# Attention scores of the four head pairs in two 64-row halves of the array, with one transposed copy of q and k

## The chip, the cores and the metric

One core of a Trainium2 chip runs the whole program. The metric is the device time of one execution in microseconds (us); lower is better. The engines have one queue of instructions each: TensorE (PE) multiplies, with a separate row of weight loads (PEld) in the profile; VectorE (DVE) and ScalarE (ACT) work element by element; GpSimd (POOL) does little here; SyncE (SP) issues the weight transfers. Matmul results land in PSUM, eight banks of 128 partitions by 512 fp32.

## The reference

Two transformer layers on 512 tokens of width 1024, in fp32. The first layer's attention is the one that changes: eight heads, each with two components of 64 features, whose softmaxes are subtracted.

```python
def diff_attention(h, cos, sin, w_qkv, q_norm, k_norm, lam_p, subln, w_o, layer_idx):
    q, k, v = jnp.split(h @ w_qkv, [DA_QK, 2 * DA_QK], axis=-1)
    q = apply_rope(rms_norm(q.reshape(B, S, DA_HEADS, 2, HEAD_DIM), q_norm), cos, sin)
    k = apply_rope(rms_norm(k.reshape(B, S, DA_HEADS, 2, HEAD_DIM), k_norm), cos, sin)
    ...
        s = jnp.einsum('bqhcd,bkhcd->bhcqk', qblk, k).astype(jnp.float32) * scale
        p = jax.nn.softmax(jnp.where(causal, s, NEG_INF), axis=-1)
        a = p[:, :, 0] - lam * p[:, :, 1]
        return jnp.einsum('bhqk,bkhe->bqhe', a.astype(v.dtype), v)
    ...
    o = rms_norm(o, subln) * (1.0 - lambda_init)
    return o.reshape(B, S, DA_V) @ w_o
```

Then come a SwiGLU FFN, the second layer (a window attention of 16 query heads on four shared key heads, window 128) and its FFN.

## The kernel before

Every product is made of two parts per operand, a value rounded to fp32r (hi, the suffix h) and the rest (lo, l), and of three matmuls, hi x hi, hi x lo and lo x hi. A split is a ScalarE cast to hi and a VectorE subtraction for lo; weights pass through it too (`parts`, L278 and L279).

The tokens are four blocks of 128. The first layer's heads go by pairs: `Pair` p has two heads, so four 64-feature components for q and four for k. For each pair `gemm` makes 512 columns of q and k for all blocks (L300 to L302 into four acc banks), then 256 of v. `rope` on VectorE turns a block's 512 columns into td, and multiplies the k half by its gains and norms into kd (L417), with each component of k twice, the second copy made by ScalarE (L419). The pair's steps are then:

- K (`turn_k`): four transposes of kd (L426) and their split into kT (L447 ScalarE, L448 VectorE).
- Q (`turn_q`): two transposes of td and their split into q (L436, L437, two steps each of 64 partitions), which stacks a component's hi above its lo in 128 rows; then the next block's rope.
- C (`score`): per component two matmuls, stacked q against kT hi twice (L809) and against kT lo twice (L810). One sc bank takes two components of up to 256 columns, or one of 384 or 512. Then VectorE adds the mask and takes the row maximum (L814, with a second short instruction, both named mx in the waits). The last C of a block starts `soften`: exponentials on ScalarE (L827), sums and the subtraction of the second softmax on VectorE (L835).
- U (`turn`): transposes of the weights (L851) and their split (L306, L307). W (`weigh`): the products with v. N (`norm`) and B (`spread`): the rms norm over heads and its way back.

The order of TensorE's work is written by hand: `DA_STEPS` gives each step a slot, `DA_STEPS3` for the last pair, and between two steps the loop pulls as many matmuls of the next pair's q, k and v (for the last pair, of the output projection) as the slots' distance times `DA_FILL` allows. ScalarE's and VectorE's order comes from priorities: a block under `tc.high_priority(offset=...)` is put ahead by that offset (BOOST for weight splits, EVAC for splits and reductions out of PSUM, HOT and NPRI for others). A pair's last steps run inside the next pair's.

PSUM has four acc banks, two tr banks for everything transposed (and for two of the FFN's sums), one sc and one po. Whoever takes a bank waits until its last reader is done. The second layer's attention has its own `score` (L1120, L1121), with the same stacked q and the sc bank, and its own list of slots (`SW_AT`, six for each of 16 units).

Of the kernel before, what the change touches and what calls it, by code (L numbers as in the profile page):

```python
# [9 lines left out]
F32 = mybir.dt.float32  # L10
# [7 lines left out]
P = 128  # L18
# [11 lines left out]
BOOST = 40  # L30
HOT = 610
EVAC = 20
# [6 lines left out]
NPRI = 1538  # L39
DA_FILL = 0.6361  # L40


def DA_STEPS(K, Q, C, U, W, N, B):
    return [
        (0, Q, 0),
        (0, K, 0),
        (5, C, 0, (0, 1)),
        (5.3, K, 1),
        (5.4, Q, 1),
        (6.5, C, 0, (2, 3)),  # L50
        (7.8, K, 2),
        (9.1, C, 1, (0, 1)),
        (11, C, 1, (2, 3)),
        (12.3, Q, 2),
        (13.5, U, 0, 1),
        (16.8, C, 2, (0,)),
        (17.5, U, 0, 0),
        (17.8, C, 2, (1,)),
        (18.4, K, 3),
        (19, C, 2, (2,)),  # L60
        (19, Q, 3),
        (20, C, 2, (3,)),
        (21, U, 1, 0),
        (21, C, 3, (0,)),
        (21.1, W, 0, 0),
        (23.1, U, 1, 1),
        (24.5, C, 3, (1,)),
        (28.5, W, 0, 1),
        (29, C, 3, (2,)),
        (30.5, N, 0),  # L70
        (31.9, C, 3, (3,)),
        (32.5, U, 2, 0),
        (38.3, B, 0),
        (38.8, U, 2, 1),
        (41.8, U, 3, 0),
        (42.8, U, 3, 1),
        (43, W, 1, 0),
        (43.1, W, 1, 1),
        (49, N, 1),
        (58.9, B, 1),  # L80
    ]


def DA_STEPS3(K, Q, C, U, W, N, B):
    return [
        (0, K, 0),
        (0, Q, 0),
        (3, K, 1),
        (3, C, 0, (0, 1)),
        (5, Q, 1),  # L90
        (6, C, 0, (2, 3)),
        (8, K, 2),
        (10, C, 1, (0, 1)),
        (12.5, C, 1, (2, 3)),
        (13, Q, 2),
        (13.5, U, 0, 0),
        (14.5, C, 2, (0,)),
        (15, U, 0, 1),
        (16.2, C, 2, (1,)),
        (18.5, K, 3),  # L100
        (19, C, 2, (2,)),
        (19, Q, 3),
        (20.3, C, 2, (3,)),
        (21.6, C, 3, (0,)),
        (22.4, U, 1, 1),
        (23.5, U, 1, 0),
        (25, C, 3, (1,)),
        (26.3, W, 0, 0),
        (27.3, W, 0, 1),
        (28.3, C, 3, (2,)),  # L110
        (30.9, N, 0),
        (31.4, C, 3, (3,)),
        (35.8, U, 2, 1),
        (38.2, U, 2, 0),
        (38.3, B, 0),
# [3 lines left out]
        (42.8, W, 1, 1),  # L119
        (48.5, N, 1),  # L120
        (57.5, B, 1),
# [3 lines left out]
DA_FILL3 = 0.468  # L125
# [22 lines left out]
def tile_yoco_hybrid(  # L148
# [44 lines left out]
    def att(tag="tr"):  # L193
        return ps.tile([P, 512], F32, name=nm(tag), tag=tag, bufs=2 if tag == "tr" else 1)
# [1095 lines left out]
```

## Time and profile before

| | us |
|---|---|
| median of 3 runs (lowest, highest) | 1179.5 (1178.88, 1181.27) |
| the profiled execution | 1179.42 |
| its span, first to last instruction | 1177.6 |
| PE busy | 1141.6 |
| DVE busy | 858.3 |
| ACT busy | 599.7 |

In time, the stages are: the start and the first pair's projections up to 46 us; the four pairs' attention from 46 to 258; the first FFN up to 635; the second layer's projections and attention from 635 to 822; the second FFN to the end. A matmul's row in the trace is longer than the distance to the next, since they are pipelined: 512 columns show 0.39 us and start 0.23 apart. So busy time of PE is not work at its peak, and distances between starts say more than durations. Idle time ahead of an instruction is put down to the wait that ended last.

### The profile page before, as it was taken

How to read it: one execution, taken by the hardware profiler on the slowest of the kernel's cores; microseconds unless marked ns; L12 is line 12 of the kernel's file. 1: busy time of each engine (PE TensorE's matmuls, PEld its weight loads, DVE VectorE, ACT ScalarE, POOL GpSimd, SP SyncE). 2: the span in 40 equal slices, each digit the busy share in tenths (PEclk: the TensorE clock that was granted, in tenths of full speed). 3: DMA queues.
4: the chain of work that ended last, by engine and by line, in shares of the span. 5: the costliest groups of instructions: out<-in, count | busy, mean ns of one | idle time of the engine just before them, and what ended most of it. 6: DMA issues, size and time to landing. Idle time of an engine off the chain costs nothing.

```text
span 1177.6 us, 16518 instructions
## 1 busy us (share of the span) xinstructions
PE 1141.6 (97%) x5910; PEld 963.7 (82%) x5910; DVE 858.3 (73%) x2084; ACT 599.7 (51%) x1259; POOL 16.9 (1%) x32
## 2 busy tenths in 40 slices
PE   8999999899999999999999999989999999999998
PEld 7888788678988888888888888767988888888887
DVE  5989898979776477467567697988777568468446
ACT  6676756554434343343346579788443343344333
POOL 0100000000000000000002000000000000000000
PEclk9999999999999999999999999999999999999999
DMA  6311121113524215206302211120605206305301
GB/s 189 108 54 55 54 61 62 59 54 86 183 74 144 70 57 178 89 1 216 106 1 75 90 58 51 37 72 1 222 29 193 94 1 210 94 19 179 108 1 71
DMA packets 86579, 103.14 MB, mean 88 GB/s; under 512 B 5161, under 2 KB 68034, under 8 KB 86498
## 3 DMA queue, kind: packets, MB, share of 16 engines
q1 hardware_dynamic: 86064, 100.97, 26.7%
q0 software_dynamic: 384, 1.11, 0.4%
q8 instruction: 46, 0.75, 0.3%
q14 instruction: 35, 0.29, 0.1%
q10 hardware_dynamic: 50, 0.01, 0.0%
HBM read 99.98 MB, written 2.10 MB: 87 GB/s over the span
## 4 chain that ended last, share of the span: by engine, by line
PE 75%; DVE 14%; ACT 7%; DMA 2%; issue 1%; SPq 0%; DVEq 0%; ACTq 0%
PE acc L300 17%; PE acc L302 17%; PE acc L301 17%; PE acc L597 15%; PE tr L597 3%; ACT s L1139 2%; DVE q L437 1%; ACT s L1146 1%; DVE s L814 1%; DMA raw<-in_da_w_qkv_dram 1%; DVE hss L393 1%; DVE lo L279 1%; DVE kT L448 1%; DVE td L412 1%; DVE u L409 1%
## 5 line engine op out<-in xcount | busy, mean ns | idle before, releaser
L301 PE MATMUL acc<-hTl,hi 128*128 128x512 f32 (+1 forms) x768 | 285.4, 372 | 1.2 <-DVE hTl L307 1.2
L300 PE MATMUL acc<-hTh,hi 128*128 128x512 f32 (+1 forms) x768 | 285.5, 372 | 0.0
L302 PE MATMUL acc<-hTh,lo 128*128 128x512 f32 (+1 forms) x768 | 285.2, 371 | 0.0
L278 ACT CAST hi<-raw 128x512 fp32r<-128x512 f32 x256 | 154.5, 621 | 249.8 <-PE acc L301 119.9
L279 DVE TENSOR_TENSOR lo<-raw,hi 128x512 fp32r<-128x512 f32 x256 | 172.9, 687 | 104.5 <-ACT hi L278 104.0
L578 ACT CAST hi<-g 128x512 fp32r<-128x512 f32 x154 | 95.6, 622 | 160.6 <-PE acc L301 99.2
L301 PEld LDWEIGHTS acc<-hTl,hi 128*128 128x128 f32 x768 | 144.7, 188 | 26.6 <-DVE hTl L307 1.7
L300 PEld LDWEIGHTS acc<-hTh,hi 128*128 128x128 f32 x768 | 144.7, 188 | 24.9
L302 PEld LDWEIGHTS acc<-hTh,lo 128*128 128x128 f32 x768 | 144.7, 188 | 24.9
L579 DVE TENSOR_TENSOR lo<-g,hi 128x512 fp32r<-128x512 f32 x154 | 104.6, 687 | 70.6 <-ACT hi L578 70.6
L300 PE MATMUL acc<-hi,hTh 128*128 128x256 f32 (+1 forms) x384 | 137.5, 358 | 3.6 <-ACT hTh L306 1.5
L302 PE MATMUL acc<-hi,hTl 128*128 128x256 f32 (+1 forms) x384 | 130.5, 340 | 0.3 <-DVE hTl L307 0.2
L301 PE MATMUL acc<-lo,hTh 128*128 128x256 f32 (+1 forms) x384 | 130.2, 339 | 0.0
L597 PE MATMUL acc<-hi,al 128*128 128x512 f32 x264 | 102.9, 390 | 0.1
L597 PE MATMUL acc<-hi,ah 128*128 128x512 f32 x264 | 102.9, 390 | 0.0
L597 PE MATMUL acc<-lo,ah 128*128 128x512 f32 x264 | 102.7, 389 | 0.0
L300 PEld LDWEIGHTS acc<-hi,hTh 128*128 128x128 f32 x384 | 73.7, 192 | 9.7 <-ACT hTh L306 1.7
L302 PEld LDWEIGHTS acc<-hi,hTl 128*128 128x128 f32 x384 | 73.3, 191 | 9.4 <-DVE hTl L652 0.7
L301 PEld LDWEIGHTS acc<-lo,hTh 128*128 128x128 f32 x384 | 73.6, 192 | 5.0 <-DVE lo L279 0.5
L606 DVE TENSOR_TENSOR xs<-xs,acc 128x512 f32<-128x512 f32 (+1 forms) x98 | 65.6, 671 | 8.1 <-PE acc L597 6.4
L517 DVE TENSOR_TENSOR sg<-sg,acc 128x512 f32<-128x512 f32 x44 | 30.2, 686 | 54.4 <-PE acc L302 54.4
L597 PEld LDWEIGHTS acc<-hi,al 128*128 128x128 f32 x264 | 49.6, 188 | 11.2 <-DVE al L535 0.9
(209 smaller groups left out, 1852.1 us busy)
## 6 DMA issues: line engine op xcount, KB each, us to landing
raw<-in_w_gate_up_dram SPq DMA_DIRECT2D x88, 512.0 KB, 3.5
g<-in_w_down_dram SPq DMA_DIRECT2D x88, 256.0 KB, 5.0
raw<-in_da_w_qkv_dram SPq DMA_DIRECT2D x30, 256.0 KB, 3.0
raw<-in_da_w_qkv_dram SPq DMA_DIRECT2D x8, 512.0 KB, 3.5
raw<-in_da_w_o_dram SPq DMA_DIRECT2D x8, 512.0 KB, 3.6
raw<-in_sw_w_q_dram SPq DMA_DIRECT2D x8, 512.0 KB, 3.5
raw<-in_sw_w_o_dram SPq DMA_DIRECT2D x8, 512.0 KB, 3.6
raw<-in_w_kv_dram SPq DMA_DIRECT2D x4, 512.0 KB, 3.4
```

What stands on the lines that cost most here:

```text
L278: nc.scalar.copy(hi, part)
L279: nc.vector.tensor_tensor(lo, part, hi.bitcast(F32), op=ALU.subtract)
L300: nc.tensor.matmul(dst, sh, mh, start=start, stop=False)
L301: nc.tensor.matmul(dst, sh, ml, start=False, stop=False)
L302: nc.tensor.matmul(dst, sl, mh, start=False, stop=stop)
L393: nc.vector.tensor_reduce(out=ss[:, t, :], in_=sq.rearrange("p (g e) -> p g e", e=HD), axis=AX.X, op=ALU.add)
L517: nc.vector.tensor_tensor(sg, sg, pu, op=ALU.mult)
L578: nc.scalar.copy(hi, src)
L579: nc.vector.tensor_tensor(lo, src, hi.bitcast(F32), op=ALU.subtract)
L597: nc.tensor.matmul(bank[t], l[:, left, tk], r, start=fresh and i == 0 and n == 0, stop=i == len(qs) - 1 and n == 2, skip_group_check=not f ...
L606: nc.vector.tensor_tensor(xs[:, tok, cs], xs[:, tok, cs], bank[t][:, c0:c0 + w], op=ALU.add)
L1139: nc.scalar.activation(sb[:, g, 0:n], sb[:, g, 0:n], AF.Exp, bias=mx[:, g:g + 1], scale=qscl[:, g:g + 1], accum_out=sm[:, g:g + 1])
```

## The change

In the pairs' attention q and k stay as `rope` leaves them, two components of a head in 128 rows. One step T (`flip`) takes the place of K and Q: four transposes of td (two of q, two of k) into one bank and one split into qkT, with the same two instructions that made kT. The gain on k is multiplied in place, and there is no kd. The stacked q is gone in this stage. C works by head: for each of its two components three matmuls of 64 rows (hi x hi, hi x lo, lo x hi), the first component in rows 0 to 63 and the second in rows 64 to 127, alternating, each component into a bank of its own. The products lo x lo, which the stacked form had, are no longer made. C has two calls a block, where it had two for the first two blocks and four for the last two. The sc bank joins the tr banks to a ring of three, also for the second layer's scores. The tables of slots, the fill factors and the offsets have new numbers.

```diff
-BOOST = 40
-HOT = 610
-EVAC = 20
+BOOST = 42
+HOT = 1220
+EVAC = 17
...
-NPRI = 1538
-DA_FILL = 0.6361
+NPRI = 759
+DA_FILL = 0.65
...
+        (0, T, 0),
+        (5, C, 0, 0),
+        (5.4, T, 1),
+        (5.78, C, 0, 1),
+        (7.16, C, 1, 0),
+        (11, C, 1, 1),
+        (11.9, T, 2),
...
     def att(tag="tr"):
-        return ps.tile([P, 512], F32, name=nm(tag), tag=tag, bufs=2 if tag == "tr" else 1)
+        return ps.tile([P, 512], F32, name=nm(tag), tag=tag, bufs=3 if tag == "tr" else 1)
...
         q, k = td[:, 0:w - nk * HD], td[:, w - nk * HD:w]
+        if nk and not twice:
+            k3 = k.rearrange("p (g e) -> p g e", e=HD)
+            nc.vector.tensor_tensor(k3, k3, kscl.unsqueeze(2).to_broadcast([P, nk, HD]), op=ALU.mult)
+            return td
...
-        def turn_k(self, i):
-            k_evac(self.kT, i, turn_cols(self.td[i][1], 4))
-
-        def turn_q(self, i):
-            self.q[i] = q_evac(self.ap, turn_cols(self.td[i][0], 2))
+        def flip(self, i):
+
+            k_evac(self.qkT, i, turn_cols(self.td[i], 4))
             self.rope(i + 1)
 
-        def score(self, i, gs):
+        def score(self, i, h):
...
-            pt = att("sc")
-            for x, g in enumerate(gs):
-                gq = slice(g * P, (g + 1) * P)
-                c = slice(x * 256, x * 256 + n)
-                nc.tensor.matmul(pt[:, c], q[:, gq], self.kT[0][:, g, 0:n], start=True, stop=False)
-                nc.tensor.matmul(pt[:, c], q[:, gq], self.kT[1][:, g, 0:n], start=False, stop=True)
...
+            pts = [att() for _ in range(2)]
+            tk = slice(i * P, (i + 1) * P)
+            for a, b in ((0, 0), (0, 1), (1, 0)):
+                for c in range(2):
+                    rows = slice(c * HD, (c + 1) * HD)
+                    nc.tensor.matmul(pts[c][:, 0:n], self.qkT[a][rows, h, tk], self.qkT[b][rows, 2 + h, 0:n],
+                                     start=a + b == 0, stop=a == 1)
+            for c in range(2):
                 with tc.high_priority(offset=pri["evac"]):
                     nc.vector.tensor_tensor_reduce(
-                        out=self.sb[i][g // 2][:, g % 2, 0:n], in0=pt[:, c], in1=maskD[:, 512 - n:512], scale=1.0,
-                        scalar=-3e38, op0=ALU.add, op1=ALU.max, accum_out=self.mx[:, g:g + 1])
-            if gs[-1] == 3:
+                        out=self.sb[i][h][:, c, 0:n], in0=pts[c][:, 0:n], in1=maskD[:, 512 - n:512], scale=1.0,
+                        scalar=-3e38, op0=ALU.add, op1=ALU.max, accum_out=self.mx[:, 2 * h + c:2 * h + c + 1])
+            if h == 1:
                 self.soften(i)
...
-            pt = att("sc")
+            pt = att()
```

The first place is on TensorE, in the second pair: the two score calls of its first token block and the turns of its second (tr, sc and acc are banks; the scores of the first two components, on sc_1394, stand just ahead of these rows). Before:

```order
L300 MATMUL acc_1351<-hi_1313,hTh_106 128x512
L301 MATMUL acc_1351<-lo_1314,hTh_106 128x512
L302 MATMUL acc_1351<-hi_1313,hTl_107 128x512
L426 MATMUL tr_1404<-ident,kd_1296 128x128 x4
L426 MATMUL tr_1411<-ident,td_1289 128x128 x2
L300 MATMUL acc_1352<-hi_1313,hTh_106 128x512
L301 MATMUL acc_1352<-lo_1314,hTh_106 128x512
L302 MATMUL acc_1352<-hi_1313,hTl_107 128x512
L809 MATMUL sc_1433<-kT_1062,q_1283 128x128
L810 MATMUL sc_1433<-kT_1063,q_1283 128x128
L809 MATMUL sc_1433<-kT_1062,q_1283 128x128
L810 MATMUL sc_1433<-kT_1063,q_1283 128x128
```

Now, from the second matmul of the first call on:

```order
L795 MATMUL tr_1366<-qkT_1030 128x128
L795 MATMUL tr_1365<-qkT_1031,qkT_1030 128x128
L795 MATMUL tr_1366<-qkT_1031,qkT_1030 128x128
L795 MATMUL tr_1365<-qkT_1030,qkT_1031 128x128
L795 MATMUL tr_1366<-qkT_1030,qkT_1031 128x128
L414 MATMUL tr_1375<-ident,td_1287 128x128 x4
L795 MATMUL tr_1391<-qkT_1030 128x128
L795 MATMUL tr_1392<-qkT_1030 128x128
L795 MATMUL tr_1391<-qkT_1031,qkT_1030 128x128
L795 MATMUL tr_1392<-qkT_1031,qkT_1030 128x128
L795 MATMUL tr_1391<-qkT_1030,qkT_1031 128x128
L795 MATMUL tr_1392<-qkT_1030,qkT_1031 128x128
```

The two calls stand with the turns alone between them, where six accumulating products stood as well, and a call is six matmuls on two banks instead of four on one.

The second place is on VectorE, in the same pair, at the scores of the third token block (384 columns; lo with raw and hi is a weight split, aT a split of turned weights of the softmax, ISA the reduction and its short second instruction). Before:

```order
L279 TENSOR_TENSOR lo_1814<-raw_1807,hi_1813 128x512
L448 TENSOR_TENSOR kT_1063<-tr_1579,kT_1062 128x4x128
L814 ISA s_1558,mx_1555<-sc_1586,maskD 128x384
L814 ISA mx_1555 128x1
L437 TENSOR_TENSOR q_1593<-tr_1590,q_1593 64x2x128
L279 TENSOR_TENSOR lo_2032<-raw_2028,hi_2031 128x512
L437 TENSOR_TENSOR q_1593<-tr_1590,q_1593 64x2x128
L814 ISA s_1558,mx_1555<-sc_1601,maskD 128x384
L814 ISA mx_1555 128x1
L307 TENSOR_TENSOR aT_1567<-tr_1621,aT_1566 128x2x128
L823 SCALAR_TENSOR_TENSOR mx_1555<-mx_1555,hscl_1047 128x4
```

Now:

```order
L799 ISA s_1526,mx_1524<-tr_1529,maskD 128x384
L799 ISA mx_1524 128x1
L263 TENSOR_TENSOR lo_1760<-raw_1753,hi_1759 128x512
L263 TENSOR_TENSOR lo_2001<-raw_1997,hi_2000 128x512
L436 TENSOR_TENSOR qkT_1031<-tr_1544,qkT_1030 128x4x128
L291 TENSOR_TENSOR aT_1519<-tr_1554,aT_1518 128x2x128
L799 ISA s_1527,mx_1524<-tr_1559,maskD 128x384
L799 ISA mx_1524 128x1
L799 ISA s_1527,mx_1524<-tr_1560,maskD 128x384
L799 ISA mx_1524 128x1
L808 SCALAR_TENSOR_TENSOR mx_1524<-mx_1524,hscl_1015 128x4
```

The two steps on q are gone, the weight splits stand ahead of the turned block's split, and the last head's two reductions follow each other.

## Rows read from the trace of the kernel before

**Rows 1.** The head of the profile page, and TensorE's line of its first part: busy us, share of the span, instructions.

```profile
span 1177.6 us, 16518 instructions
...
PE 1141.6 (97%) x5910; PEld 963.7 (82%) x5910; DVE 858.3 (73%) x2084; ACT 599.7 (51%) x1259; POOL 16.9 (1%) x32
```

**Rows 2.** Busy time by stretch: the stretch and its length, busy us and instructions of PE, PEld, DVE, ACT and POOL, then granted clock, DMA share and GB/s. The pairs' attention and the first FFN.

```profile
46.00:258.00 212.00, 198.41 (x1195) 167.96 (x1194) 189.64 (x636) 137.43 (x346) 1.56 (x3) 0.99 0.18 56
...
290.00:635.00 345.00, 344.97 (x1611) 289.02 (x1610) 227.37 (x380) 138.25 (x230) 0.21 (x1) 1.00 0.31 101
```

**Rows 3.** The chain of waits from 46 to 258 us, its shares by engine and line (the line is as long as the view prints it).

```profile
by line: PE acc L300 8.3%; PE acc L301 7.8%; PE acc L302 7.7%; DVE s L814 6.1%; DVE q L437 5.0%; DVE kT L448 4.5%; ACT s L827 3.7%; PE sc L809 3.6%; DVE lo L279 3.3%; DVE aT L307 3.3%; DVE u L409 2.8%; DVE s L835 2.7%; PE po L879 2.6%; issu
```

**Rows 4.** The list of waits from 46 to 258 us, TensorE's weight loads: who waited for whom, us in total, times, longest.

```profile
PEld tr L426 <- ACT kd L419: 5.5, 6, 1.6
PEld sc L809 <- DVE mx L814: 5.5, 13, 1.2
PEld sc L809 <- ACT kd L419: 2.8, 2, 1.4
```

**Rows 5.** TensorE in order of time, four places in the second pair's scores, one for each width: start us, us, engine, line, operation, out<-in.

```profile
108.04 0.22 PE L809 MATMUL sc<-kT,q 128*128 128x128 f32 x1
108.10 0.28 PE L810 MATMUL sc<-kT,q 128*128 128x128 f32 x1
108.21 0.27 PE L809 MATMUL sc<-kT,q 128*128 128x128 f32 x1
...
110.93 0.28 PE L810 MATMUL sc<-kT,q 128*128 128x256 f32 x1
111.05 0.40 PE L300 MATMUL acc<-hi,hTh 128*128 128x512 f32 x1
...
118.34 0.34 PE L810 MATMUL sc<-kT,q 128*128 128x384 f32 x1
118.51 0.40 PE L300 MATMUL acc<-hi,hTh 128*128 128x512 f32 x1
...
126.80 0.39 PE L810 MATMUL sc<-kT,q 128*128 128x512 f32 x1
127.03 0.28 PE L300 MATMUL po<-aT,vh 128*128 128x256 f32 x1
```

**Rows 6.** TensorE around the 9-row turn at the start, in order of time: matmuls first, then weight loads, with the idle time ahead in brackets.

```profile
10.48 0.39 PE L302 MATMUL acc<-hi,hTl 128*128 128x512 f32 x1
10.80 0.22 PE L236 MATMUL tr<-ident,grow 9*128 9x9 f32 x1
...
11.29 0.39 PE L301 MATMUL acc<-lo,hTh 128*128 128x512 f32 x1
...
10.80 0.13 PEld L236 LDWEIGHTS tr<-ident,grow 9*128 9x128 f32 x1 [0.36 <-issue]
10.95 0.19 PEld L300 LDWEIGHTS acc<-hi,hTh 128*128 128x128 f32 x1
11.06 0.19 PEld L301 LDWEIGHTS acc<-lo,hTh 128*128 128x128 f32 x1
```

**Rows 7.** Groups of instructions from 46 to 258 us by shape: busy us, mean ns of one, idle us before.

```profile
L437 DVE TENSOR_TENSOR q<-tr,q 64x256 fp32r<-64x256 f32 x32 | 13.5, 422 | 1.0
L417 DVE TENSOR_TENSOR kd<-td,hscl 128x256 f32<-128x256 f32 x15 | 6.3, 420 | 0.2
L436 ACT CAST q<-tr 64x256 fp32r<-64x256 f32 x32 | 11.8, 368 | 15.5 <-DVE q L437 10.5 <-PE tr L426 4.7
L419 ACT COPY kd<-kd 128x256 f32<-128x256 f32 x16 | 6.4, 402 | 1.7 <-DVE kd L417 1.3 <-DVE rsq_t L257 0.2
```

**Rows 8.** VectorE, ScalarE and TensorE around one wait for kd in the first pair, each in order of time.

```profile
55.39 0.42 DVE L437 TENSOR_TENSOR q<-tr,q 64x256 fp32r<-64x256 f32 x1
55.84 0.42 DVE L417 TENSOR_TENSOR kd<-td,hscl 128x256 f32<-128x256 f32 x1
...
56.35 0.40 ACT L419 COPY kd<-kd 128x256 f32<-128x256 f32 x1
...
55.30 0.40 PE L302 MATMUL acc<-hi,hTl 128*128 128x512 f32 x1
56.81 0.66 PE L426 MATMUL tr<-ident,kd 128*128 128x128 f32 x4 [1.12 <-ACT kd L419]
```

**Rows 9.** VectorE in order of time ahead of a reduction that TensorE waits for, in the second pair.

```profile
124.15 0.42 DVE L437 TENSOR_TENSOR q<-tr,q 64x256 fp32r<-64x256 f32 x1
124.60 0.69 DVE L279 TENSOR_TENSOR lo<-raw,hi 128x512 fp32r<-128x512 f32 x1
125.32 0.43 DVE L437 TENSOR_TENSOR q<-tr,q 64x256 fp32r<-64x256 f32 x1
```

**Rows 10.** VectorE in order of time at two 128-column reductions: the first, and the short instruction that ends the second.

```profile
107.07 0.29 DVE L814 CUSTOM_DVE_ANT_0 s<-sc,maskD 128x128 f32<-128x128 f32 x1
...
107.57 0.08 DVE L814 DVE_READ_ACCUMULATOR2_ANT mx<- 128x1 f32 x1
```

**Rows 11.** The list of waits from 685 to 822 us, the second layer's attention: weight loads that waited for the score bank's reduction.

```profile
PEld sc L1120 <- DVE mx L1126: 3.7, 5, 1.8
```

**Rows 12.** Busy time by stretch, with the columns of rows 2: the last pair's longest pause of TensorE and the stretch behind it.

```profile
250.16:252.54 2.38, 0.40 (x3) 0.03 (x1) 2.38 (x8) 2.38 (x8) 0.00 (x0) 1.00 0.00 0
253.70:257.10 3.40, 3.40 (x14) 3.11 (x13) 2.71 (x8) 1.05 (x4) 0.00 (x0) 0.50 0.24 74
```

More of the change, by code (lines that the diff above doesn't have):

```diff
@@ L78, in DA_STEPS, with DA_STEPS3 @@
         (43.1, W, 1, 1),
-        (49, N, 1),
+        (47.84, N, 1),
         (58.9, B, 1),
     ]
-def DA_STEPS3(K, Q, C, U, W, N, B):
+def DA_STEPS3(T, C, U, W, N, B):
     return [
[L86 to L95, printed above, removed]
+        (0, T, 0),
+        (3, C, 0, 0),
+        (5, T, 1),
+        (6, C, 0, 1),
+        (10, C, 1, 0),
+        (12.5, C, 1, 1),
+        (13, T, 2),
         (13.5, U, 0, 0),
-        (14.5, C, 2, (0,)),
         (15, U, 0, 1),
[L99 to L104, printed above, removed]
+        (16.2, C, 2, 0),
+        (19, T, 3),
+        (20.3, C, 2, 1),
         (22.4, U, 1, 1),
         (23.5, U, 1, 0),
-        (25, C, 3, (1,)),
+        (25, C, 3, 0),
         (26.3, W, 0, 0),
         (27.3, W, 0, 1),
-        (28.3, C, 3, (2,)),
         (30.9, N, 0),
-        (31.4, C, 3, (3,)),
+        (31.4, C, 3, 1),
         (35.8, U, 2, 1),
-        (38.2, U, 2, 0),
-        (38.3, B, 0),
+        (36.16, B, 0),
+        (37.1, U, 2, 0),
         (39.4, U, 3, 0),
@@ L401, in head_stats, with rope @@
         return scl3
-    def rope(ap, t, groups, turns, stretch, nk, kscl):
+    def rope(ap, t, groups, turns, stretch, nk, kscl, twice=True):
         w = groups * HD
@@ L787, in stretch @@
                 return td, z, Cd[:, i].unsqueeze(2).to_broadcast([P, 2, 2, P])
[L789 to L795 removed]
+            self.td[i] = rope(self.ap, t, 8, turns, stretch, 4, self.scl[:, i, 4:8], False)
+        def flip(self, i):
+            k_evac(self.qkT, i, turn_cols(self.td[i], 4))
             self.rope(i + 1)
[L798 removed]
+        def score(self, i, h):
             n = (i + 1) * P
[L800 removed]
+            if h == 0:
                 self.mx = small([P, 4], "mx")
@@ L900, in steps @@
         def steps(self):
-            K, Q, C, U, W, N, B = (self.turn_k, self.turn_q, self.score, self.turn, self.weigh, self.norm, self.spread)
-            return (DA_STEPS3 if self.p == 3 else DA_STEPS)(K, Q, C, U, W, N, B)
+            T, C, U, W, N, B = self.flip, self.score, self.turn, self.weigh, self.norm, self.spread
+            return (DA_STEPS3 if self.p == 3 else DA_STEPS)(T, C, U, W, N, B)
     with tc.tile_pool(name="da", bufs=1, reuse_waits="tile") as ap:
```

50 lines of the change are left out of this document (15 added, 35 removed).

## The prediction

> **What bounds the kernel now.** The page's first part comes first: TensorE is busy for 97% of the span [rows 1]. Such a share is a mean over stages, so the table by stage is next [rows 2]. In the first FFN TensorE has 344.97 of 345 us in work: nothing beside it counts there. The stretch that the change rewrites, 46 to 258 us (the four pairs), is another: TensorE 198.4 of 212 us, VectorE 189.6. Two engines are nearly full there, and each waits for the other. The chain of waits over that stretch says the same: it passes from the accumulating products to VectorE's small steps and back, and the q split alone (L437) is 5.0% of it, 10.6 us [rows 3]. What TensorE's weight loads wait for is in the list of waits [rows 4]: ScalarE's second copy of k (kd, 8.3 us in eight waits) and the score bank that VectorE hasn't yet reduced (mx, 5.5 us in thirteen). So I sum from TensorE's side: work taken out and put in, waits taken out and put in.
>
> **The change part by part.**
>
> *Turns.* Six 128-column turns a token block become four: 32 turns fewer. Matmuls of 128 columns stand 0.11 us apart, and so do their weight loads [rows 5, 6]. 32 x 0.11 = **-3.5 us**, all on TensorE.
>
> *Scores.* Before, 128 full-height matmuls, 32 of each width. From start to start they take 0.11 us (108.10 to 108.21), 0.12 (110.93 to 111.05), 0.17 (118.34 to 118.51) and 0.23 (126.80 to 127.03) for 128, 256, 384 and 512 columns [rows 5]: 32 x 0.63 = 20.2 us. Now there are 192 of half height. The trace has no two matmuls in two halves of the array. If each pair costs what one full-height matmul does, 96 slots are 24 x 0.63 = 15.1 us; if each costs that by itself, 30.2. Between them lies a third value: weight loads stand 0.11 us apart (10.95 and 11.06) [rows 6], and at 128 columns it is they that space the matmuls, since after a pause two start 0.06 apart (108.04, 108.10) [rows 5]. If two products stream side by side but their loads go one after the other, a pair takes at least 0.22: 24 x (0.22 + 0.22 + 0.22 + 0.23) = 21.4. I take halfway between 15.1 and 21.4, 18.3: the two halves write different banks and share no row, so I hold the streams to be parallel, while a load's 9-row form (0.13 us) is not much shorter than the 128-row one (0.19) [rows 6], so for the loads the rows decide nothing. **-1.9 us** (ends -5.1 and +10.0).
>
> The Trainium skill, "TensorEngine Tiling (Array Packing)", section "Tiling Modes", says that tiles run weight loads and matmuls independently, in parallel. By it the scores would be the 15.1, and the sum 3.2 us lower. No row here shows it.
>
> *Changes of height.* The array takes a lower operand once inside the stream: the 9-row turn L236. Its load is held for 0.36 us with nothing named; from the matmul ahead (10.48) to the second one behind it (11.29) are 0.81 us, where two 512-column steps of 0.227 and one turn of 0.11 would be 0.56 [rows 6]. So going low and back costs about 0.25 us. There are 32 score calls, and in the new order full-height work stands between all of them: 32 x 0.25 = 8.0. Where TensorE waits ahead of a call anyway, the way in is hidden; I take off a quarter: **+6.0 us** (ends 0, and 32 x 0.36 = 11.5).
>
> *kd and the q split.* VectorE loses 32 steps of 0.42 us, 13.5 us; ScalarE 32 of 0.37 and 16 of 0.40, 18.2 us [rows 7]. The k gain's multiplication stays, in place (kd L417 becomes a td step of the same size). On the path: the matmul that starts at 55.30 is the last until 56.81, where kd has come. Ahead of it VectorE does q (55.39), kd (55.84), then ScalarE copies (56.35 to 56.75) [rows 8]. Without q and the copy that is 0.45 + 0.5 us less; times eight waits, 7.6 of the 8.3. What feeds the turn is still a VectorE step behind others, so I take **-5.0 us** (ends 0, -8.3).
> At 124 to 126.5 the reduction that frees the score bank stands behind q, lo, q [rows 9]; the second order table of the change shows the new row, where both q are gone and the two reductions of a head stand together. Half of the 5.5 us of mx waits: **-2.5 us** (ends 0, -5.5).
>
> *The ring.* A score call now takes two of three banks that the turns use too. In the first order table the two calls of a pair's first block have only one turn group between them, where six accumulating products and a turn group stood. The second call needs both reductions of the first: two 128-column ones take 0.58 us (107.07 to 107.65) [rows 10], about 0.3 after the matmul record's start, and 0.44 of turns lie over that. With the handover I put 0.6 a pair: **+2.4 us** (ends 0, and 4 x 1.2, the longest mx wait [rows 4]). Behind the waiting matmul on TensorE stand six accumulating products of the next pair, and the block's softmax on the other two engines waits for the reductions that follow.
>
> *At nothing, with ends.* The second attention block keeps its stacked q, only its bank comes from the ring: mx waits are 3.7 us there [rows 11]; 0, ends -3.7 and +3.7. The other numbers (orders, offsets of HOT, BOOST, EVAC, NPRI) move VectorE's and ScalarE's steps; in the FFNs TensorE's full row covers them [rows 2], and without that cover a late bank costs one step of 0.69 us [rows 9]. The granted clock is 0.50 (1.2 GHz) from 253.7 to 257.1, behind a stretch of 2.4 us in which TensorE had 0.4 us of work [rows 12]; if that pause shrinks, the fall may go too and give back half of 3.4 us, or a new one cost as much: 0, ends -1.7 and +1.7.
>
> **The sum:** -3.5 - 1.9 + 6.0 = +0.6 of work; -5.0 - 2.5 + 2.4 = -5.1 of waits; together -4.5. The profiled execution took 1179.4 us (its span 1177.6 [rows 1], and 1.8 around it), 0.1 us under the median of 1179.5; so **1175.0 us**.
>
> **The rivals.**
> *A, loads side by side as well.* Scores at 15.1 (-5.1), all of the kd waits gone (-8.3): -3.5 - 5.1 + 6.0 - 8.3 - 2.5 + 2.4 = -11.0, 1168.5 us. For it: eight kd waits with one cause. Against: VectorE's 189.6 us of work would still be 176. The Trainium skill's section "Tiling Modes", quoted under the scores from its page "TensorEngine Tiling (Array Packing)", speaks for this case.
> *B, no gain.* Loads in series (+1.2) and every change of height paid (8.0): -3.5 + 1.2 + 8.0 - 5.0 - 2.5 + 2.4 = +0.6, 1180.1 us. For it: the held load is a row, and TensorE has only 13.6 us without a matmul in the stretch, so added work shows at once. Against: some calls wait anyway.
> The Trainium skill, same page, section "PSUM Bottleneck", says that tiling speeds up the array but not the evacuation of its banks. The row that bears on it is the reduction: 64 of them before and 64 after, at the same widths.
> *C, slower: the halves do not run side by side.* The change then doesn't do what it says: scores 30.2 (+10.0), -3.5 + 10.0 + 6.0 - 5.0 - 2.5 + 2.4 = +7.4, 1186.9 us. It decides from a pair's spacing: at 22.8 us for 96 pairs, 0.24 a pair, the forecast's gain is gone, and at 0.26 the kernel is slower by more than 0.2%. For it: every matmul in this trace starts after the one ahead has streamed. Against: no two of them use different rows.
>
> **How the numbers follow.** Forecast 0.40 (1171 to 1179), A 0.18, B 0.22, C 0.20. Two parts in a thousand, 2.4 us, is about what a measurement can tell from no change. Faster by more: 0.30 of the forecast's, all of A, 0.02 of B: 0.50. Within: 0.09 and 0.14: 0.23. Slower: 0.01, 0.06 and C's 0.20: 0.27. The range goes from 1167.5 (A's lower part left out) to 1187.5 (C's upper part), some 0.16 outside.
>
> **What would show it.** Starts of the two matmuls of a pair a few hundredths apart, and pairs of 512 columns 0.23 apart: streams parallel; pairs of 128 columns 0.11 or 0.22 apart settles the loads. The load row ahead of a call and behind it: the height changes. In the list of waits kd gone, and what stands for td. The start of a pair's second score call: the ring. Wrong would be above all a pair spacing over 0.24, height changes over 0.36 a call, or VectorE's share of 46 to 258 us staying at nine tenths.

## The result and the profile after

| | before | after |
|---|---|---|
| median, us (lowest to highest) | 1179.19 (1177.07 to 1181.27) | 1165.12 (1164.05 to 1166.75) |
| profiled execution, us | 1179.4 | 1164.5 |
| its span, us | 1177.6 | 1162.6 |
| mean granted clock in it | 0.997 | 1.000 |

The changed kernel takes 0.9882 of the time before (95% interval 0.986 to 0.9904): 14.1 us less, where 4.5 were forecast. It lies below the range.

To see where, I cut the span of each profiled execution at the same instructions: the first turn of a pair's block, the first turn of normed rows (xn), the first and last product of the FFN's down half, the first turn of the second layer's FFN. The parts that belong to the two FFNs (36.3, 301.6 and 357.2 us) are equal to a tenth. The others, and the places where the granted clock is 0.50 for 3.4 us:

| stage, us | before | after | change |
|---|---|---|---|
| start | 46.3 | 45.9 | -0.4 |
| four pairs | 231.4 | 221.1 | -10.3 |
| rest of the output product, to the 32nd xn turn | 19.2 | 17.8 | -1.4 |
| second layer's attention | 185.6 | 182.7 | -2.9 |
| stretches at half clock | at 253.7, 639.4 | none but at the end | |

The head of the page and TensorE's line, against [rows 1]: TensorE has 32 matmuls more, VectorE 32 instructions and ScalarE 48 fewer.

```profile
span 1162.6 us, 16451 instructions
...
PE 1136.0 (98%) x5942; PEld 952.5 (82%) x5942; DVE 841.5 (72%) x2052; ACT 583.9 (50%) x1211; POOL 16.5 (1%) x32
```

Busy time by stretch, columns as in [rows 2], of the pairs:

```profile
46.00:250.00 204.00, 197.83 (x1244) 161.70 (x1243) 175.86 (x607) 123.72 (x302) 1.55 (x3) 1.00 0.19 60
```

TensorE was without a matmul for 13.6 of 212 us before, and now is for 6.2 of 204. VectorE's 189.6 became 175.9, 86% of the stretch where it was 89%.

What TensorE's weight loads wait for from 46 to 258 us, against [rows 4] (who waited for whom, us in total, times, longest):

```profile
PEld acc L284 <- issue: 4.9, 16, 0.4
PEld tr L795 <- issue: 4.0, 13, 0.4
PEld tr L795 <- DVE qkT L436: 2.0, 3, 0.7
...
PEld tr L795 <- DVE mx L799: 0.9, 2, 0.5
```

The copy of k (8.3 us) is gone, and an unreduced bank holds the score calls for 0.9 us where it was 5.5 (which part of the change did that, the runs below tell). New are loads held with nothing named, 13 times ahead of a score call (L795) and 16 times behind one (L284), up to 0.4 us each: the changes of height. In order of time 31 of the 32 calls start 0.07 to 0.10 us later than the matmul ahead of them needs. New as well is the wait for the turned q and k (L436), in three third blocks. The chain of waits over the pairs, 46 to 250 us, no longer holds a q step, against [rows 3]:

```profile
by line: PE acc L284 10.5%; PE acc L286 9.2%; PE acc L285 9.2%; DVE s L799 6.4%; DVE lo L263 6.1%; PE tr L795 5.3%; DVE s L820 3.8%; DVE hss L377 3.5%; PE po L285 3.4%; DVE u L393 3.4%; DVE qkT L436 3.0%; PE po L286 2.7%; PE po L864 2.6%; i
```

One 512-column score call in order of time: matmuls first, then weight loads, to be read beside [rows 5, 6].

```profile
81.36 0.40 PE L286 MATMUL acc<-hi,hTl 128*128 128x512 f32 x1
81.69 0.50 PE L795 MATMUL tr<-qkT 64*128 64x512 f32 x2
82.03 0.62 PE L795 MATMUL tr<-qkT,qkT 64*128 64x512 f32 x4
82.58 0.39 PE L284 MATMUL acc<-hi,hTh 128*128 128x256 f32 x1
...
81.69 0.19 PEld L795 LDWEIGHTS tr<-qkT 64*128 64x128 f32 x2 [0.36 <-issue]
81.80 0.42 PEld L795 LDWEIGHTS tr<-qkT,qkT 64*128 64x128 f32 x4
82.58 0.19 PEld L284 LDWEIGHTS acc<-hi,hTh 128*128 128x128 f32 x1 [0.36 <-issue]
```

Six products of 512 columns are through in 0.89 us (81.69 to 82.58). One after another at 0.227 they would need 1.36. The two of a pair start some 3 ns apart (in some calls of 384 columns, 30), and pairs follow each other at 0.11, 0.11, 0.17 and 0.23 us for the four widths (the first pair of a call takes about 0.1 longer). So streams and weight loads both go side by side.

### The profile page after: what moved, and what is told of

It is laid out like the page before. It is cut to its first block, busy times and chain, and to the rows that moved or that the text cites. A ratio compares the mean times of both kernels' runs of the same rounds, so it can differ in the third digit from the quotient of the medians.

```text
span 1162.6 us, 16451 instructions
## 1 busy us (share of the span) xinstructions
PE 1136.0 (98%) x5942; PEld 952.5 (82%) x5942; DVE 841.5 (72%) x2052; ACT 583.9 (50%) x1211; POOL 16.5 (1%) x32
## 4 chain that ended last, share of the span: by engine, by line
PE 78%; DVE 14%; ACT 5%; DMA 2%; issue 1%; SPq 0%; DVEq 0%; ACTq 0%
PE acc L284 18%; PE acc L286 18%; PE acc L285 18%; PE acc L585 15%; PE tr L585 3%; DVE lo L263 1%; ACT s L1124 1%; DVE hss L377 1%; DVE s L799 1%; PE tr L795 1%; DVE u L393 1%; ACT s L1131 1%; PE po L285 1%; PE tr L302 1%; DMA raw<-in_da_w_qkv_dram 1%
## 5 line engine op out<-in xcount | busy, mean ns | idle before, releaser
L284 PE MATMUL acc<-hTh,hi 128*128 128x512 f32 (+1 forms) x768 | 285.5, 372 | 0.0
L284 PEld LDWEIGHTS acc<-hTh,hi 128*128 128x128 f32 x768 | 144.6, 188 | 24.9
L284 PE MATMUL acc<-hi,hTh 128*128 128x256 f32 (+1 forms) x384 | 137.5, 358 | 4.9 <-ACT hTh L290 1.6
L284 PEld LDWEIGHTS acc<-hi,hTh 128*128 128x128 f32 x384 | 72.9, 190 | 15.7 <-issue 3.7
L585 PEld LDWEIGHTS acc<-hi,al 128*128 128x128 f32 x264 | 49.5, 188 | 11.1 <-DVE al L523 0.9
```

The lines of the kernel that those rows point to most:

```text
L284: nc.tensor.matmul(dst, sh, mh, start=start, stop=False)
L585: nc.tensor.matmul(bank[t], l[:, left, tk], r, start=fresh and i == 0 and n == 0, stop=i == len(qs) - 1 and n == 2, skip_group_check=not f ...
```

## The experiments

Each was timed beside the kernel before on one chip. "Over after" is against the median of 1165.12 us. Ratios are to the kernel before, whose own median beside the runs was 1179.1 to 1180.0 us, so "over after" is good to about 1 us. Times of stages are those of the profiled execution.

One thing holds for several of these figures. The changed kernel's profiled execution has no stretch at half clock before its end. Those of the runs that put back the turns, the k copy or the q steps have one or two in the second layer, which these edits do not touch, and that stage takes 1.4 to 1.8 us more in them. So about that much of each "over after" there belongs to the clock and not to the step put back.

### Do the halves pay by running side by side?

By component: one half's three products, then the other's.

```diff
-            for a, b in ((0, 0), (0, 1), (1, 0)):
-                for c in range(2):
+            for c in range(2):
+                for a, b in ((0, 0), (0, 1), (1, 0)):
```

> The changed kernel, with the three products of one component issued before the three of the other, so that only one in six matmuls can start beside one of the other half: 160 slots in place of 96, 25 us of scores in place of 15. If TensorE's work sets the pace of the pairs' stage now: plus 8 to 10 us, 1173 to 1175. If VectorE still sets it: plus 0 to 4, 1165 to 1169. If the halves never ran side by side: no change.

1173.14 us, 0.9947 (0.9933 to 0.996), 8.0 over after. But the products did not go one after another: the same call as above, in order of time, looks as before, and its second half's matmuls start within 10 ns of the first half's, though they stand three later in the program.

```profile
81.67 0.50 PE L795 MATMUL tr<-qkT 64*128 64x512 f32 x2
82.00 0.63 PE L795 MATMUL tr<-qkT,qkT 64*128 64x512 f32 x4
82.56 0.39 PE L284 MATMUL acc<-hi,hTh 128*128 128x256 f32 x1
...
106.10 0.32 PE L795 MATMUL tr<-qkT 64*128 64x128 f32 x1
106.26 0.38 PE L795 MATMUL tr<-qkT,qkT 64*128 64x128 f32 x2
106.92 0.33 PE L795 MATMUL tr<-qkT 64*128 64x128 f32 x1 [0.28 <-DVE mx L799]
107.09 0.38 PE L795 MATMUL tr<-qkT,qkT 64*128 64x128 f32 x2
```

Only where the second bank isn't reduced yet (106.92) does each half stand alone. So this run says nothing on running in series. Its profiled execution, 1176.6 us, is its slowest, 3.4 above the median; against the changed kernel's it loses 7.9 us in the pairs (229.0), 2.8 in the second layer (185.5) and 1.4 between, with three stretches at half clock. The longest, in busy time by stretch (stretch, length, TensorE's, its loads', VectorE's, ScalarE's and GpSimd's busy us, clock, DMA share, GB/s), follows a pause in which TensorE worked 1.60 of 3.40 us:

```profile
249.80:253.20 3.40, 1.60 (x7) 0.94 (x6) 0.28 (x2) 2.13 (x4) 0.00 (x0) 1.00 0.77 282
253.20:263.40 10.20, 10.05 (x28) 7.98 (x28) 4.58 (x14) 1.37 (x3) 0.00 (x0) 0.50 0.36 112
```

Both products of a pair in the same 64 rows, so that a head's second component gets the first one's scores:

```diff
-                    rows = slice(c * HD, (c + 1) * HD)
+                    rows = slice(0, HD)
```

> The changed kernel with all half-height products taken from rows 0 to 63, so that the second head of each pair gets the first one's scores: its output is not the reference's. Same instructions, same banks, same order; only the rows of the second head's operands differ. Theory: it is the rows that let two products run side by side. Here they cannot: a pair takes 0.22 to 0.46 us where it took 0.11 to 0.23, 15.1 us more on TensorE for 96 pairs, 1174 to 1182 us. Rival: it is the two banks that let them, and the time stays within 2 us of the changed kernel's.

1178.89 us, 0.9988 (0.9979 to 0.9997), 13.8 over after. This is the comparison in series. A 512-column call in order of time:

```profile
84.53 0.73 PE L795 MATMUL tr<-qkT 64*128 64x512 f32 x2
85.11 1.08 PE L795 MATMUL tr<-qkT,qkT 64*128 64x512 f32 x4
86.11 0.39 PE L284 MATMUL acc<-hi,hTh 128*128 128x256 f32 x1
```

1.58 us where it was 0.89. The banks are the same two: it is the rows that let the matmuls run together. The pairs take 232.9 us (11.8 more), the second layer 185.5 with two stretches at half clock. Over all 32 calls the products take some 15 us longer than in the changed kernel, and the kernel 13.8. With the halves in series the whole change would be worth about 1 us.

### What does a change of height cost?

Twins on the kernel before: one extra 128-column product at the head of each of its 48 score calls in the pairs, once with 64 rows, once with 128.

```diff
+            nc.tensor.matmul(pt[:, 0:P], q[0:HD, 0:P], self.kT[0][0:HD, 0, 0:P], start=True, stop=True)
```

```diff
+            nc.tensor.matmul(pt[:, 0:P], q[:, 0:P], self.kT[0][:, 0, 0:P], start=True, stop=True)
```

> The kernel before, with one extra matmul of 64 rows and 128 columns ahead of each of its 48 score calls, overwritten by the call's first product: 48 changes of height and back, and 48 x 0.11 us. If a change and back costs 0.4 us as the starts in the changed kernel say: 48 x 0.4 = 19 over the full-height twin e11_full_height_extra, or 10 to 15 where waits hide a third. If it costs the 0.25 that the forecast took: 6 to 12 over the twin.

> The twin of e10_half_height_extra with the extra matmul at full height (128 rows, 128 columns): 48 x 0.11 = 5.3 us at most, 1180 to 1185 us, by any theory; less where TensorE waits anyway.

1191.31 us, 1.0098 (1.0084 to 1.0111), and 1188.70, 1.0071 (1.0055 to 1.0086). Both expectations were missed: the full-height twin lies above the 1185 that it was given by any theory, and the two differ by 2.6 us where at least 6 were expected. The second twin has four stretches at half clock where the first has two, and its score calls wait 9.6 us for an unreduced bank where the first one's wait 5.2, so part of the height's cost falls into waits, and the times don't price the change. The stream does. TensorE in order of time around one extra product (L806), first of the half-height twin:

```profile
109.12 0.39 PE L302 MATMUL acc<-hi,hTl 128*128 128x512 f32 x1
109.44 0.32 PE L806 MATMUL sc<-kT,q 64*128 64x128 f32 x1
...
110.19 0.44 PE L300 MATMUL acc<-hi,hTh 128*128 128x512 f32 x1
```

And of the full-height twin:

```profile
107.93 0.39 PE L302 MATMUL acc<-hi,hTl 128*128 128x512 f32 x1
108.16 0.22 PE L806 MATMUL sc<-kT,q 128*128 128x128 f32 x1
...
108.66 0.45 PE L300 MATMUL acc<-hi,hTh 128*128 128x512 f32 x1
```

From the matmul ahead to the next 512-column product: 1.07 us and 0.73. Low and back costs 0.34 us, where I had read 0.25 from [rows 6]. Where the calls wait for nothing else, the same comparison gives 0.33 to 0.35 at 128, 384 and 512 columns.

### The turns

Two of the four turned again, so that there are six a block:

```diff
-            k_evac(self.qkT, i, turn_cols(self.td[i], 4))
+            k_evac(self.qkT, i, turn_cols(self.td[i], 4, 2))
```

> The changed kernel, with two of the four turns of each block made twice into the same place: the 32 turns of 0.11 us that the change took out are back, and nothing else. If TensorE's work sets the pace: plus 3.5 us, 1168 to 1169. If VectorE does: plus 0 to 1, 1165 to 1166.

1168.05 us, 0.9905 (0.9892 to 0.9919), 2.9 over after. In the profiled execution, 3.7 us over the changed kernel's, 1.6 of it is in the pairs (222.7) and 1.8 in the second layer, with two stretches at half clock there.

### The k copy and the q split

The multiplied k goes through a buffer and is copied back by ScalarE:

```diff
-            nc.vector.tensor_tensor(k3, k3, ..., op=ALU.mult)
+            nc.vector.tensor_tensor(kd.rearrange("p (g e) -> p g e", e=HD), k3, ..., op=ALU.mult)
+            nc.scalar.copy(k, kd)
```

> The changed kernel, with one ScalarE copy of k (0.40 us, 128x256) put back between the k gain's multiplication and the turns, so that each block's turns wait for VectorE and then ScalarE. Relief theory: the eight old waits for kd held 8.3 us; they come back in part, 3 to 6 us, 1168 to 1171 us. Theory two: the new slots leave the turns late enough, at most 1 us, 1165 to 1166.

1168.10 us, 0.9907 (0.9894 to 0.9921), 3.0 over after.

The four q steps of a block put back, reading td, so that no bank is held (nothing uses their result):

```diff
+                for own in (slice(0, HD), slice(HD, P)):
+                    nc.scalar.copy(q[own, 0:256], self.td[i][own, 0:256])
+                    nc.vector.tensor_tensor(q[own, 256:512], self.td[i][own, 0:256], ..., op=ALU.subtract)
```

> The q split's work put back into the changed kernel as in e1_q_split_back, but reading td in SBUF, so that no bank of the ring waits for it. If e1's 20 us are the time of VectorE and ScalarE themselves: plus 10 to 20, 1175 to 1185 us. If they are mainly banks of the ring held longer: plus 3 to 7, 1168 to 1172. If the ring explains all of it: plus 0 to 2.

1173.86 us, 0.9959 (0.9947 to 0.9972), 8.7 over after.

The same steps reading the turn bank, behind the split of q and k:

```diff
+            pt = turn_cols(self.td[i], 4)
+            k_evac(self.qkT, i, pt)
+            q_evac(self.ap, pt)
```

> The changed kernel, with the old split of q put back behind the new split, 32 ScalarE casts of 0.37 us and 32 VectorE steps of 0.42 us, on a tile that nobody reads; TensorE's work is the same. Theory one (relief): the change gained because TensorE no longer waits behind these steps, so most of VectorE's 13.5 us shows: 5 to 10 us over the changed kernel, 1170 to 1175 us. Theory two (orders, ring and offsets gained it, the relief is minor): at most 2 us, 1165 to 1167.

1184.99 us, 1.0047 (1.0034 to 1.0059), 19.9 over after, where the theory with the most gave 10. That is 11.1 us beyond the steps' own 8.7. The profiled execution is at half clock for 20.4 us before its end, where the one above is for 10.2, so by estimate up to half of that difference, 5 us, is the clock's. The rest goes with the bank that is held longer: on this ring the longer hold of one bank cost some 6 us by that estimate.

### Orders and offsets

```diff
-BOOST = 42
-HOT = 1220
-EVAC = 17
+BOOST = 40
+HOT = 610
+EVAC = 20
...
-NPRI = 759
+NPRI = 1538
```

> The changed kernel with the old priority offsets (BOOST 40, HOT 610, EVAC 20, NPRI 1538): TensorE's order is the same, VectorE's and ScalarE's differ. Relief theory: 0 to plus 2 us, 1165 to 1167. Theory two (orders and offsets): plus 3 to 8, 1168 to 1173.

With BOOST, HOT, EVAC and NPRI of before: 1168.78 us, 0.9903 (0.989 to 0.9916), 3.7 over after.

```diff
-        (5.78, C, 0, 1),
-        (7.16, C, 1, 0),
+        (6.5, C, 0, 1),
+        (9.1, C, 1, 0),
...
-DA_FILL3 = 0.4757
+DA_FILL3 = 0.468
```

> The changed kernel with the old tables' slots and fill factors for the pairs (a T at the old turn of q, a head's scores at the slot of its second component); the second layer's slots stay new. If the new pair slots carry part of the gain beyond relief and ring: plus 2 to 5 us, 1167 to 1170. If not: within 1.5 us of 1165.

With the slots that the pairs had before, and DA_FILL likewise: 1171.79 us, 0.9935 (0.9922 to 0.9947), 6.7 over after, more than expected. The pairs take 224.7 us, with a stretch at half clock in them.

```diff
-        (19, T, 3),
+        (18.2, T, 3),
```

> The changed kernel with the turns of the last block 0.8 slots earlier in the first three pairs, so that 0.5 us more of accumulating products lies between them and the second score call of the third block, which waits 0.8 to 0.9 us for the split of that turn in each of these pairs. If that wait is a pure loss: minus 0.8 to 2.5 us, 1162.5 to 1164.5. If the turns then wait for their own operand instead: 0 to plus 1.

The last block turned a little earlier, for the L436 waits: 1165.00 us, 0.9875 (0.9862 to 0.9889), no different from the changed kernel. The pairs gain 2.4 us (218.7). The next stage gives back 0.8 of it, and a new stretch at half clock in the second layer 1.5 more.

### The ring

The changed kernel with two banks for turns and one apart for scores:

```diff
-        return ps.tile([P, 512], F32, name=nm(tag), tag=tag, bufs=3 if tag == "tr" else 1)
+        return ps.tile([P, 512], F32, name=nm(tag), tag=tag, bufs=2 if tag == "tr" else 1)
...
-            pts = [att() for _ in range(2)]
+            pts = [att("sc"), att()]
...
-            pt = att()
+            pt = att("sc")
```

> The changed kernel with the old banks: two for turns and one sc, which the first component's scores and the second layer's scores take, the second component's taking a turn bank. If the ring of three gave part of the gain: plus 3 to 8 us, 1168 to 1173. If the gain is relief alone: plus 0 to 2, 1165 to 1167.

1177.37 us, 0.9977 (0.9968 to 0.9987), 12.3 over after, above both theories: pairs 225.7, second layer 189.3.

The ring alone in the kernel before, all else as it was (the second place stands twice, for the scores of either layer):

```diff
-        return ps.tile([P, 512], F32, name=nm(tag), tag=tag, bufs=2 if tag == "tr" else 1)
+        return ps.tile([P, 512], F32, name=nm(tag), tag=tag, bufs=3 if tag == "tr" else 1)
...
-            pt = att("sc")
+            pt = att()
```

> The kernel before with the ring alone: three banks for turns and scores of both layers, all else as it was. Relief theory: the score bank's waits of 5.5 and 3.7 us fall in part, minus 0 to 4 us, 1175 to 1179. If the ring is the main source: minus 5 to 10, 1169 to 1174. If its order of sharing costs: plus 1 to 4.

1176.41 us, 0.9976 (0.9966 to 0.9987), 3.1 less than the 1179.48 beside it: pairs 227.9, second layer 186.7. Faster, where the prediction put the ring at a loss.

The same, and the second layer's new slots (SW_AT, SW_R):

```diff
-SW_R = [-0.4, 13.7, 12.7, 39.5, 43.9, 51.8]
+SW_R = [-0.4, 13.7, 14.24, 39.07, 43.47, 47.06]
```

> The kernel before, with the one ring of three banks (as in the run before_with_ring) and the second layer's new slots (SW_AT, SW_R); pairs untouched. The ring alone gave 2.8 us: 3.5 in the pairs, and 1.1 lost in the second layer. Theory: the second layer's slots are what the ring needs there; that stage falls from 186.7 us to 183 to 185 and the kernel takes 1172.5 to 1174.5 us. Rival: the slots only fit the other pairs, the stage stays at 186 to 187, and the kernel takes 1176 to 1177 us.

1173.11 us, 0.9947 (0.9934 to 0.9961): 6.9 less than the 1180.03 of the kernel before beside it, without a half-height product. Its waits over the pairs, 46 to 258 us:

```profile
PEld tr L426 <- ACT kd L419: 6.7, 6, 1.6
PEld tr L809 <- ACT kd L419: 3.5, 2, 1.8
...
PEld tr L809 <- DVE mx L814: 0.8, 4, 0.2
```

And over the second layer's attention, 670 to 822 us:

```profile
PEld tr L1120 <- DVE mx L1126: 1.1, 1, 1.1
```

The waits for an unreduced bank fall from 5.5 to 0.8 us [rows 4] and from 3.7 to 1.1 [rows 11]. The wait for the k copy grows meanwhile, from 8.3 to 10.2.

The changed kernel with the second layer's old slots:

```diff
-SW_R = [-0.4, 13.7, 14.24, 39.07, 43.47, 47.06]
+SW_R = [-0.4, 13.7, 12.7, 39.5, 43.9, 51.8]
```

(SW_AT likewise.)

> The changed kernel with the second layer's old slots (SW_AT, SW_R). Theory: the second layer's 2.9 us come from slots and ring together, so that stage goes from 182.7 back to about 185 to 187 us and the kernel takes 1167.5 to 1169.5 us. Rival: the stage gained because a fall of the clock is gone by chance; it stays at 182.7 to 184.5 and the kernel takes 1165 to 1167 us.

1170.88 us, 0.9919 (0.9907 to 0.9932), 5.8 over after. The second layer takes 188.3 us, more than either theory gave. Over the kernels of this part and the next one that stage reads (in brackets the stretches at half clock in it, 3.4 us each):

| second layer's attention, us | full height: bank apart | full height: ring | half height: bank apart | half height: ring |
|---|---|---|---|---|
| old slots | 185.6 (1) | 186.7 (1) | 186.7 (2) | 188.3 (2) |
| new slots | not run | 182.7 (0) | 189.3 (1) | 182.7 (0) |

Either alone loses, with no more stretches at half clock than the kernel that it is read against; both together gain, and of that gain (2.9 and 4.0 us) the one or two stretches that are gone can be as much as half their length, 1.7 or 3.4.

### The square

The changed kernel's half height without the ring of three and without the second layer's new slots. As in the run with the score bank apart, a call needs two banks, and its second one is one of the two turn banks; the second layer's scores go back to the bank apart:

```diff
-        return ps.tile([P, 512], F32, name=nm(tag), tag=tag, bufs=3 if tag == "tr" else 1)
+        return ps.tile([P, 512], F32, name=nm(tag), tag=tag, bufs=2 if tag == "tr" else 1)
...
-            pts = [att() for _ in range(2)]
+            pts = [att("sc"), att()]
...
-            pt = att()
+            pt = att("sc")
...
-SW_R = [-0.4, 13.7, 14.24, 39.07, 43.47, 47.06]
+SW_R = [-0.4, 13.7, 12.7, 39.5, 43.9, 51.8]
```

> The changed kernel with one score bank apart from the ring (as in the run score_bank_apart: two banks for turns, one for scores, the second product of a pair in a turn bank) and with the second layer's old slots. It closes the square: the kernel before; before with ring and new second-layer slots (1173.1 us, 6.9 less); this one, half height without either; the changed kernel, which has both. Theory: half height and ring with slots are two gains that nearly add up. The second layer goes from 189.3 us back to 185 to 186, so 1172.5 to 1175 us, 5 to 7.5 less than before. Rival: half height needs the ring, and without it the second layer's slots make no difference: 1176 to 1178.5 us, and the ring's worth in the changed kernel stays above 11 us.

1174.01 us, 0.9958 (0.9945 to 0.9972), 5.3 less than the 1179.31 before. In the second layer its scores wait as in the kernel before, 3.7 us in five waits for the reduction [rows 11]:

```profile
PEld sc L1105 <- DVE mx L1111: 3.7, 5, 1.8
```

In the pairs, 46 to 258 us, it is otherwise: the score calls wait 0.5 us for an unreduced bank, without the ring. What waits is the turns of the softmax weights (L836):

```profile
PEld tr L836 <- issue: 5.4, 5, 2.5
...
PEld tr L836 <- DVE mx L799: 1.3, 1, 1.3
...
PEld sc L795 <- DVE mx L799: 0.5, 1, 0.5
```

The list names nothing for the 5.4 us, but the order of time does for the longest of these pauses: the turns start when the splits of earlier turns (aT) have read their bank.

```profile
246.96 0.63 PE L836 MATMUL tr<-ident,s 128*128 128x128 f32 x4 [2.10 <-DVE aT L291]
```

With the ring the changed kernel has none of the 5.4 us; its turns of weights wait 2.5 us in all.

| median less than before, us | bank apart, old second-layer slots | ring, new second-layer slots |
|---|---|---|
| full height, old orders | 0 | 6.9 |
| half height, new orders | 5.3 | 14.1 |

The two gains add up to 12.2 of 14.1. The ring alone, with the second layer's old slots, is worth 3.1 us at either height: 1179.5 to 1176.4 in the kernel before, and 1174.0 to 1170.9 here.

Full height on all that is new (k copied, q split, products of 128 rows, the changed kernel's orders, offsets and ring):

```diff
+                    nc.tensor.matmul(pts[c][:, 0:n], q[:, gq], self.qkT[z][:, g, 0:n], start=z == 0, stop=z == 1)
```

> The changed kernel's ring, orders, slots and offsets, but with the scores in full height as before: k multiplied and copied into kd, six turns a block, q split in halves from a ring bank of its own, four products of 128 rows for each pair of heads, two banks a call. Theory 1, the half-height path itself is what pays: the waits that went with the k copy and the q split (10.9 us) come back, less 2.3 us of work on TensorE that the halves added, so 1172 to 1182 us, with the pairs' stage at 229 to 239 us. Theory 2, the ring, the slots and the offsets carry the gain: within 3 us of the changed kernel, 1164 to 1168.

1184.64 us, 1.0032 (1.0021 to 1.0044), 19.5 over after, above the first theory's range. The old path on the new orders is worse than the kernel before. Its waits over the pairs, 46 to 260 us, show why:

```profile
PEld tr L797 <- DVE qkT L436: 6.5, 8, 1.2
PEld tr L414 <- ACT kd L407: 5.5, 3, 4.0
PEld tr L414 <- DVE mx L800: 3.2, 4, 1.2
```

The old path's own steps are what TensorE waits for: the split behind the turns, the k copy, and banks that are not yet reduced. So the pairs' new orders, with two banks a call, do not pay with the old path.

## Why the prediction was wrong

The direction was right. Without its ring term the forecast was -6.9 us, and the half-height kernel without the ring gained 5.3; that it came so near is in part luck, since its terms missed in both directions. **The step that failed is the ring**, put at +2.4, with the second layer, which shares it, at nothing: measured, the ring alone is -3.1 us, and with the second layer's slots -6.9 to -8.9.

*Turns, -3.5.* Putting the two extra turns back cost 2.9 us, of which the pairs show 1.6 and the clock in the second layer most of the rest: the size is near, but not cleanly shown.

*Scores, -1.9.* The low end, -5.1, was it: loads as well as streams go side by side. I had taken halfway because no row showed two loads at once. What the Trainium skill's "TensorEngine Tiling (Array Packing)" says in its section "Tiling Modes", which has tiles load and multiply independently, agrees with the pairs' spacing of 0.11 us.

*Changes of height, +6.0.* Undersized: 0.34 a call, so 32 x 0.34 = 10.9 if no call hides it; 29 held loads of up to 0.4 us (13 in, 16 out) stand in the list of waits, few calls wait for anything else, and taking a quarter off was not borne out. The two errors on TensorE's work nearly cancel, by luck: -3.5 - 5.1 + 10.9 = +2.3, forecast +0.6.

*kd, q and mx waits, -5.0 and -2.5.* The half-height kernel without the ring gained 5.3 though it had 2.3 us more work, so waits and all else in that kernel gave 7.6 us, where 7.5 were forecast. This is a difference, and its parts are not as forecast. By its list of waits the kd waits are gone whole (8.3, where 5.0 were credited) and the score calls' wait for an unreduced bank went from 5.5 to 0.5 (where 2.5 were); against that, TensorE waits 2.6 us for the turned q and k, and 6.7 at the turns of the softmax weights, where it was 3.1. Undone one by one in the changed kernel, the k copy costs 3.0 us and the q steps 8.7, together more than the forecast's 5.0 for both; why was not separated.

*The ring, +2.4, and the second layer, 0.* Measured -3.1 for the ring alone at either height, and with the second layer's slots -6.9 at full height and -8.9 at half height (1174.0 to 1165.1). I costed what sharing takes: a pair's second call that needs both reductions of the first. That wait exists in one call of the 32, 0.29 us at 53.63, with 0.22 more inside the call until the second bank is free (53.85), and one turn waits 0.9 us for a bank:

```profile
53.63 0.54 PE L795 MATMUL tr<-qkT 64*128 64x128 f32 x2 [0.29 <-DVE mx L799]
53.85 0.33 PE L795 MATMUL tr<-qkT,qkT 64*128 64x128 f32 x1
...
PEld tr L836 <- DVE mx L799: 0.9, 1, 0.9
```

I did not cost what sharing gives. Before, every score call had one bank and waited whenever that one was unreduced: 5.5 us in the pairs [rows 4] and 3.7 in the second layer [rows 11], both in rows that I quoted. I put the first down to VectorE's order and half-credited it, and the second to nothing. At full height, with three banks in the ring, those waits go to 0.8 and 1.1 with no change to what VectorE does. At half height the pairs' score calls have that gain without the ring (0.5 us); there the third bank serves the turns of the softmax weights, whose 5.4 us of waits are gone with it. I had no term for those: the two turn banks of the kernel before were never priced as a limit. By stage the ring and its slots gave, under half height, 3.2 us in the pairs (224.3 to 221.1), 1.5 behind them and 4.0 in the second layer (186.7 to 182.7). The 8.9 is against a kernel whose score calls take one of the two turn banks, since a call at half height needs two, and which keeps the pairs' new slots and offsets; a half-height kernel whose orders suit the bank apart was not run, so some of the 8.9 may be orders that fit the ring.

*The clock, 0 (ends -1.7 and 1.7).* The profiled run before has two stretches at half clock, the half-height kernel without the ring two, before with ring and slots none, the changed kernel none. So part of the ring's gain comes by the clock. Before with ring and slots took 1172.0, 1172.9 and 1173.1 us where the mean clock was 0.998 or more, and 1175.1 and 1176.8 where it was 0.997 and 0.996. By that, as an estimate, some 3 of the 8.9 us are clock; the two stretches lie in the second layer's stage, so most of its 4.0 us may be theirs. Ahead of both stretches of the kernel before TensorE had 1.42 and 1.68 us of work in 3.40, in the columns used above:

```profile
250.30:253.70 3.40, 1.42 (x9) 1.02 (x8) 3.40 (x9) 3.40 (x10) 0.00 (x0) 1.00 0.00 0
636.00:639.40 3.40, 1.68 (x10) 1.23 (x10) 2.04 (x3) 3.40 (x7) 2.52 (x3) 1.00 0.73 172
```

No run changed the pause alone, so that the shorter pauses are what kept the clock up is argued, not shown.

*The rivals.* A, 1168.5, came nearest, and both its premises hold (loads side by side, kd waits gone). It too had the ring at +2.4 and the heights at +6.0. B (changes of height all paid) was right on that term and wrong on the loads. C's premise is what the products in one half made true, and there 13.8 us were lost. That run's 1178.9 lies below C's 1186.9 because C too had the ring at +2.4: with -8.9 in its place C's sum is 1175.6.

*Left open.* Of the signs of being wrong that the prediction names, two did not come (pairs are 0.11 to 0.23 us apart, a change of height costs 0.34), and the third, VectorE's share, is not clear: 85% of 46 to 258 us where it was 89. It named none for a gain by the ring. The offsets cost 3.7 us when put back and the pairs' old slots 6.7. These, like the k copy and the q steps, can't be added up: with the other undoings they come to more than the 14.1 us that the whole change gained. Why 1.9 us come only with both the ring and the half height wasn't separated. Nor was the 8 us of the order by component, beyond its three stretches at half clock.

## What to carry to other kernels

When two kinds of tile are to share one ring, cost both sides, what sharing takes and what a further buffer gives to either kind. The waits for the buffer that each had to itself are already rows in the list of waits; here the scores' waits went at full height and the turns' waits at half height, and the ring with its slots, the clock included, was most of what the forecast lacked. A slot table and a ring are one change: either alone made the second layer 1.1 to 2.6 us slower than the same kernel without it. To learn what running side by side is worth, make it impossible (same rows), since a changed order alone did not undo it.

## What the runs showed of the hardware

Matmuls of two row halves overlap even when they stand in the program three of one half, then three of the other: starts 10 ns apart (81.666 and 81.676). Same banks, same order, one half: 1.58 us for six 512-column products in place of 0.89. Going from 128 rows to 64 and back costs 0.34 us, seen as loads held 0.35 to 0.36 us on either side. A stretch at half clock lasted 3.4 us in most cases, 6.8 in two runs and 10.2 in one.
